# A full-height second score product and a mask on GpSimd, in the attention of a hybrid decoder layer

## The chip, the cores and the metric

The kernel runs on one core of a Trainium2 chip. The metric is the device time of one execution in microseconds (us). Its engines appear under the profile's names: PE is TensorE (matrix products; PEld is its weight load), DVE is VectorE, ACT is ScalarE, POOL is GpSimd, SP is SyncE, which issues the loads.

## What is computed

One layer of a decoder for 512 tokens of 1,024 values, all in float32: a recurrent branch, an attention branch, an MLP and a gated embedding, each with its norm. The change touches the attention alone. It has 16 heads of 64 values, is strictly causal, and weighs the keys by stick breaking:

```python
z = einsum('bhqd,bhkd->bhqk', q_blk, k) * scale          # scale = 1/8
causal = key_pos[None, :] < q_pos[:, None]
log_1m = where(causal, log_sigmoid(-z), 0.0)
suffix = cumsum(log_1m, axis=3, reverse=True) - log_1m
att = where(causal, exp(log_sigmoid(z) + suffix), 0.0)
y = einsum('bhqk,bhkd->bhqd', att, v)
```

So the weight of a key is sigmoid(z) times the product of sigmoid(-z) over all later keys that are allowed.

## The kernel before

Float32 products are made of two float32r parts per operand, a rounded high part and the exact rest (`split`, lines 53 and 54: a copy on ACT, a subtraction on DVE). A projection (`proj`) is 24 products of 128 rows by 512 columns: 8 tiles of the contraction, three products each (lines 120 to 122). The weights stream in halves of 512 KB, three buffers deep, each split one half ahead of its use.

The heads come in 8 pairs; a pair's two heads lie on partitions 0 to 63 and 64 to 127 of one projection. For each pair there is one projection of q and one of k into PSUM. All projections share three PSUM slots (pool `pp`). `qk_evac` empties them: for head j of the pair, `qs[:, j, :]` holds the high part of q on the head's own 64 partitions and the low part on the other 64 (lines 405 and 406), `kh[:, j, :]` the high part of k on both halves (lines 407 and 408), and `kl` the low part of k, both heads in one tile, each on its own partitions (line 409). These three tiles have two buffers in turn, by pair. ACT's and DVE's reads of one PSUM tile are put in the order of the code.

`scores` handles a head's queries in four blocks of 128 (`qb`), with the keys 0 to w = 128 (qb + 1). The first product (line 419) has 128 rows, (high q, low q) against (high k, high k). The second (line 420) adds high q against low k, with the head's 64 rows only. A mask tile, 0 where allowed and -1e30 elsewhere, is added to the diagonal block of z in PSUM (line 421, DVE). Then come two sigmoids, r of -z and s of z (lines 425 and 426, ACT), a scan that multiplies r up from the last key (line 427, DVE), and s times the scan (line 429, DVE). There are 16 heads of 4 blocks, so each of these lines has 64 instructions. `values` transposes the weights of the head before (line 440), splits them and multiplies them with v (lines 449 and 450). `branch_gate` adds projections for the two branch gates (`ps_gl`, `ps_ga`); those, and the q and k projections of the next pairs, are what PE issues between the small products of a head.

The order of the instructions on each engine is not written out: the framework plans it ahead of the run, by the order of the code and a model of the durations, with the dependences and the buffers that it knows.

Of the kernel before, what the change touches and what calls it, by code (L numbers as in the profile page):

```python
# [8 lines left out]
F32 = mybir.dt.float32  # L9
F32R = mybir.dt.float32r  # L10
I32 = mybir.dt.int32
AF = mybir.ActivationFunctionType
ALU = mybir.AluOpType
PSUM = bass.MemoryType.PSUM

P = 128
S = 512
D = 1024
KT = D // P
NB = S // P  # L20
FF = 4096
HEADS = 16
DH = 64
PAIRS = HEADS // 2
EPS = 1e-6
NEG = -1.0e30
GN = 4
# [5 lines left out]
def hybrid_layer(ctx, tc, xT, pT, vecs, gfin, gates, w_in, w_bl, w_ba, w_out,  # L33
                 w_up, w_dn, w_pg, w_ple, out):
    nc = tc.nc
    sc, ve, pe, gp, sy = nc.scalar, nc.vector, nc.tensor, nc.gpsimd, nc.sync
# [6 lines left out]
    def f32(ap):  # L43
        return ap.bitcast(F32)

# [1 line left out]
    def load_raw(src, name):  # L47
# [21 lines left out]

    # half chunks of weights (1024 per partition) in the order of use, each split ahead of its use  # L70
    halves = []
# [59 lines left out]

# [1 line left out]
    vt = const.tile([P, len(VECS), 8], F32, name="vt")  # L133
# [9 lines left out]
    for a, b in ((0, 1), (1, 2), (2, 4), (4, 6), (6, 8)):  # L143
# [8 lines left out]
    sc.activation(zero, onesf[:, 0:1], AF.Copy, scale=0.0)  # L152
    mask = const.tile([P, P], F32, name="mask")
    gp.memset(mask, 0.0)
    gp.affine_select(mask, mask, pattern=[[-1, P]], compare_op=ALU.is_gt, fill=NEG,
                     base=0, channel_multiplier=1)

    # keeps the tensor engine's clock up while the first loads arrive
    with tc.tile_pool(name="warm", bufs=1, space=PSUM) as pw:
# [12 lines left out]
    def row_sums(acc, pool, name):  # L172
        """sums over the partitions of acc, tokens on the partitions: [128, NB] in PSUM"""
        ps = pool.tile([P, S], F32, tag="ps", name="sum_" + name, bufs=1)
        for tb in range(NB):
            pe.matmul(ps[:, tb:tb + 1], acc[:, tb * P:(tb + 1) * P], onesf[:, 0:1],
                      start=True, stop=True)
        return ps[:, 0:NB]

    def spread(cols, pool, dpool, name):  # L180
        """a value per token, [128, NB], to every partition: [128, S] in PSUM"""
        ps = pool.tile([P, S], F32, tag="ps", name="bc_" + name, bufs=1)
        for tb in range(NB):
            dg = dpool.tile([P, P], F32, tag="dg", name=f"dg_{name}{tb}", bufs=2)
            ve.tensor_scalar(dg, ident, cols[:, tb:tb + 1], None, op0=ALU.mult)
            pe.matmul(ps[:, tb * P:(tb + 1) * P], onesf, dg, start=True, stop=True)
        return ps

    def rsqrt_cols(y, ss, pool, name, rest=None):
        """1/sqrt(ss / D + eps), a few values per partition"""  # L190
        n = y.shape[1]
        v = pool.tile([P, n], F32, tag="nv", name="v_" + name, bufs=2)
        t = pool.tile([P, n], F32, tag="nt", name="t_" + name, bufs=2)
        yi, vi = y.bitcast(I32), v.bitcast(I32)
        ve.tensor_scalar(v, ss, 1.0 / D, EPS if rest is None else rest, op0=ALU.mult, op1=ALU.add)
        ve.tensor_scalar(yi, vi, 1, None, op0=ALU.logical_shift_right)
        ve.tensor_scalar(yi, yi, -1, 0x5F1FFFF9, op0=ALU.mult, op1=ALU.add)

        def ratio():
            if n == 1:  # L200
                ve.scalar_tensor_tensor(t, y, y, v, op0=ALU.mult, op1=ALU.mult)
            else:
                ve.tensor_tensor(t, y, y, op=ALU.mult)
                ve.tensor_tensor(t, t, v, op=ALU.mult)

        ratio()
        ve.tensor_scalar(t, t, -0.703952253, 1.68191391, op0=ALU.mult, op1=ALU.add)
        ve.tensor_tensor(y, y, t, op=ALU.mult)
        ratio()
        ve.tensor_scalar(v, t, 0.375, -1.25, op0=ALU.mult, op1=ALU.add)  # L210
        ve.tensor_tensor(t, t, v, op=ALU.mult)
        return ve.scalar_tensor_tensor(y, t, 1.875, y, op0=ALU.add, op1=ALU.mult)

# [1 line left out]
    vs = big.tile([P, PAIRS, NB, 4, DH], F32R, tag="B1", name="vs")  # L215
# [58 lines left out]

# [1 line left out]
    with tc.tile_pool(name="lru", bufs=1) as lp, \  # L276
            tc.tile_pool(name="pg", bufs=3, space=PSUM) as pgp:
        # decay constants: 8 softplus(-lam)
        sp8 = const.tile([P, 8], F32, name="sp8")
# [70 lines left out]

        # u_x
        pend = None
# [13 lines left out]
        y_lru = big.tile([P, KT, S], F32, tag="F1", name="y_lru")  # L366
        # u_g
        for n in range(KT):
# [11 lines left out]

# [1 line left out]
        w = next_pair("v3")  # L382
# [4 lines left out]

# [1 line left out]
    f2 = ctx.enter_context(tc.tile_pool(name="f2", bufs=1))  # L389
    t1 = f2.tile([P, KT, S], F32, tag="F2", name="t1")  # L390
    t2 = f2.tile([P, KT, S], F32, tag="F3", name="t2")
    yas = vs.rearrange("p a t b d -> p a (t b d)").rearrange("p a (h s) -> p a h s", h=2)
    with tc.tile_pool(name="att", bufs=2) as ap, \
            tc.tile_pool(name="pz", bufs=2, space=PSUM) as pz, \
            tc.tile_pool(name="pt", bufs=2, space=PSUM) as ptp, \
            tc.tile_pool(name="py", bufs=1, space=PSUM) as pyp:

        def qk_evac(p, psq, psk):
            qs = ap.tile([P, 2, S], F32R, tag="qs", name=f"qs{p}")
            kh = ap.tile([P, 2, S], F32R, tag="kh", name=f"kh{p}")  # L400
            kl = ap.tile([P, S], F32R, tag="kl", name=f"kl{p}")
            for j in range(2):
                a = slice(j * DH, (j + 1) * DH)
                b = slice((1 - j) * DH, (2 - j) * DH)
                sc.copy(qs[a, j, :], psq[a, :])
                ve.tensor_tensor(qs[b, j, :], psq[a, :], f32(qs[a, j, :]), op=ALU.subtract)
                sc.copy(kh[a, j, :], psk[a, :])
                sc.copy(kh[b, j, :], psk[a, :])
                ve.tensor_tensor(kl[a, :], psk[a, :], f32(kh[a, j, :]), op=ALU.subtract)
            return qs, kh, kl  # L410

        turned, summed = {}, {}     # of the last head so far: last transpose and last product, by block of keys

        def scores(p, j, qb, qs, kh, kl):
            w = (qb + 1) * P
            a = slice(j * DH, (j + 1) * DH)
            q = slice(qb * P, w)
            z = pz.tile([P, S], F32, tag="z", name=f"z{p}_{j}_{qb}")
            pe.matmul(z[:, 0:w], qs[:, j, q], kh[:, j, 0:w], start=True, stop=False)
            pe.matmul(z[:, 0:w], qs[a, j, q], kl[a, 0:w], start=False, stop=True)  # L420
            ve.tensor_tensor(z[:, q], z[:, q], mask, op=ALU.add)  # L421
            r = ap.tile([P, S], F32, tag="r", name=f"r{p}_{j}_{qb}", bufs=3)
            s = ap.tile([P, S], F32, tag="s", name=f"s{p}_{j}_{qb}", bufs=6)
            pr = ap.tile([P, S], F32, tag="pr", name=f"pr{p}_{j}_{qb}", bufs=2)
            sc.activation(r[:, 0:w], z[:, 0:w], AF.Sigmoid, scale=-0.125)  # L425
            sc.activation(s[:, 0:w], z[:, 0:w], AF.Sigmoid, scale=0.125)
            ve.tensor_tensor_scan(pr[:, 0:w][:, ::-1], r[:, 0:w][:, ::-1],  # L427
                                  zero.broadcast_to([P, w]), 1.0, op0=ALU.mult, op1=ALU.add)
            ve.tensor_tensor(s[:, 0:w - 1], s[:, 0:w - 1], pr[:, 1:w], op=ALU.mult)  # L429
            return s  # L430
# [57 lines left out]

# [1 line left out]
    pools["proj"] = pq = ctx.enter_context(tc.tile_pool(name="pq", bufs=4, space=PSUM))  # L490
# [23 lines left out]

# [1 line left out]
    sumsq = big2.tile([P, S], F32, tag="S", name="sumsq2")  # L516
# [6 lines left out]

# [1 line left out]
    rs2 = sumsq  # L525
# [9 lines left out]
    for half in range(2):  # L535
# [13 lines left out]
        if half == 0:  # L549
            # p @ w_ple, token-major, between the halves  # L550
            ple = f2.tile([P, NB, D], F32, tag="F2", name="ple")
# [30 lines left out]

# [1 line left out]
    work = big2.tile([P, 8192], F32, tag="B3", name="work")  # L584
# [40 lines left out]

    # w_ple_gate, all resident: three halves in the stream's slots, five in buffers now free
    wb1 = big.tile([P, 8, 1024], F32R, tag="B1", name="wb1")
# [24 lines left out]
def _layout(a):  # L652
    """Host layout only: tiles of 128 rows, chunks that one transfer brings in whole."""
    import numpy as np
# [67 lines left out]
```

## Time and profile before

| | |
|---|---|
| median of 3 runs | 969.02 us (968.84 to 971.86) |
| span of the profiled execution | 967.4 us |
| the three runs one by one | 971.86, 969.02, 968.84 us |
| PE busy | 951.4 us (98%) |
| DVE busy | 554.4 us (57%) |
| ACT busy | 471.9 us (49%) |
| POOL busy | 5.5 us (1%) |

The span is the time from the first to the last instruction of the one execution that was profiled; a run's time is longer by what lies around it, 1.6 us from this span to the median. Times of the trace count from the span's start. A matmul's duration in the trace overlaps with the next one's, so how fast products follow each other is read from their starts. "a <-b" in a list of waits says that b released a.

### The profile page before, as it was taken

Reading aid. Unit: us, or ns where it says so; the run is one execution under the profiler, and the core shown is the slowest. Engines: PE = TensorE matmul, PEld = TensorE weight load, DVE = VectorE, ACT = ScalarE, POOL = GpSimd, SP = SyncE. Lnnn points to the kernel's source line nnn. Section 1 sums busy time; section 2 is a strip of 40 time slices with the busy share of each in tenths; the row PEclk is TensorE's granted clock in tenths of the full one; section 3 lists DMA queues with packets and bytes.
Section 4 is the critical chain, followed back from the end, with each engine's and each line's share of the span. In section 5 each row is a group of like instructions: output and inputs, shape, how many; then the busy total and the mean of one; then the engine's idle time right before and its main releaser. Section 6 shows DMA issues by size and latency. Waiting matters only on the chain.

```text
span 967.4 us, 11858 instructions
## 1 busy us (share of the span) xinstructions
PE 951.4 (98%) x4634; PEld 789.3 (82%) x4634; DVE 554.4 (57%) x882; ACT 471.9 (49%) x751; POOL 5.5 (1%) x19
## 2 busy tenths in 40 slices
PE   7999999999999999999999999999999999999996
PEld 7988888777777777788888888888888888888896
DVE  6896847688887887553555543424343333444476
ACT  6568594656565665441324355542123545333443
POOL 0000000000000000000000000000000000000000
PEclk9999999999999999999999999999999999999998
DMA  6342323212211111243223232323323232232312
GB/s 214 94 131 66 109 66 109 88 44 66 65 66 65 67 66 44 66 174 106 90 93 103 87 109 88 111 71 123 109 87 108 88 99 98 88 104 92 109 44 88
DMA packets 25400, 89.41 MB, mean 92 GB/s; under 512 B 2944, under 2 KB 3200, under 8 KB 25088
## 3 DMA queue, kind: packets, MB, share of 16 engines
q1 hardware_dynamic: 24768, 87.61, 27.3%
q10 hardware_dynamic: 576, 1.05, 0.3%
q8 instruction: 36, 0.59, 0.3%
q14 instruction: 20, 0.16, 0.1%
HBM read 86.55 MB, written 2.10 MB: 92 GB/s over the span
## 4 chain that ended last, share of the span: by engine, by line
PE 95%; ACT 2%; DVE 1%; DMA 1%; issue 1%; SPq 0%; ACTq 0%
PE ps_up L120 6%; PE dn L122 6%; PE dn L120 6%; PE ps_up L122 6%; PE ps_up L121 6%; PE dn L121 6%; PE z L420 2%; PE t L440 2%; PE ps_k L120 2%; PE ps_gl L121 2%; PE ps_q L121 2%; PE ps_k L122 2%; PE pgt L121 2%; PE pgt L122 2%; PE ps_gl L120 2%; PE pgt L120 2%
## 5 line engine op out<-in xcount | busy, mean ns | idle before, releaser
L120 PE MATMUL dn<-ah,whi_dn 128*128 128x512 f32 x256 | 100.3, 392 | 0.0
L120 PE MATMUL ps_up<-h,whi_up 128*128 128x512 f32 x256 | 100.0, 391 | 0.0
L122 PE MATMUL ps_up<-h,wlo_up 128*128 128x512 f32 x256 | 99.8, 390 | 0.0
L122 PE MATMUL dn<-ah,wlo_dn 128*128 128x512 f32 x256 | 99.8, 390 | 0.0
L121 PE MATMUL ps_up<-h,whi_up 128*128 128x512 f32 x256 | 99.7, 390 | 0.0
L121 PE MATMUL dn<-al,whi_dn 128*128 128x512 f32 x256 | 99.7, 389 | 0.0
L53 ACT CAST whi_dn<-raw_dn 128x1024 fp32r<-128x1024 f32 x32 | 33.6, 1053 | 108.4 <-PE dn L121 82.9
L54 DVE TENSOR_TENSOR wlo_up<-raw_up,whi_up 128x1024 fp32r<-128x1024 f32 x32 | 39.2, 1224 | 73.5 <-ACT whi_up L53 73.5
L53 ACT CAST whi_up<-raw_up 128x1024 fp32r<-128x1024 f32 x32 | 33.7, 1054 | 91.4 <-PE ps_up L121 63.0
L54 DVE TENSOR_TENSOR wlo_dn<-raw_dn,whi_dn 128x1024 fp32r<-128x1024 f32 x32 | 39.0, 1222 | 67.6 <-ACT whi_dn L53 67.6
L122 PEld LDWEIGHTS dn<-ah,wlo_dn 128*128 128x128 f32 x256 | 48.1, 188 | 10.1
L122 PEld LDWEIGHTS ps_up<-h,wlo_up 128*128 128x128 f32 x256 | 48.1, 188 | 10.0
L121 PEld LDWEIGHTS ps_up<-h,whi_up 128*128 128x128 f32 x256 | 48.1, 188 | 9.9
L121 PEld LDWEIGHTS dn<-al,whi_dn 128*128 128x128 f32 x256 | 48.1, 188 | 9.9
L120 PEld LDWEIGHTS ps_up<-h,whi_up 128*128 128x128 f32 x256 | 48.1, 188 | 9.8
L120 PEld LDWEIGHTS dn<-ah,whi_dn 128*128 128x128 f32 x256 | 48.1, 188 | 9.6
L427 DVE TENSOR_TENSOR_SCAN pr<-r,zero 128x128 f32<-128x128 f32 (+1 forms) x64 | 51.7, 817 | 5.1 <-ACT r L425 4.7
L425 ACT ACTIVATE r<-z 128x128 f32<-128x128 f32 (+1 forms) x64 | 28.2, 440 | 33.5 <-DVE z L421 33.3
L575 DVE TENSOR_TENSOR d<-dn,sumsq 128x512 f32<-128x512 f32 x16 | 11.1, 692 | 52.1 <-PE dn L122 52.1
L54 DVE TENSOR_TENSOR al<-rl,ah 128x512 fp32r<-128x512 f32 x32 | 22.2, 693 | 18.2 <-ACT ah L53 18.1
L421 DVE TENSOR_TENSOR z<-z,mask 128x128 f32<-128x128 f32 x64 | 18.5, 294 | 24.4 <-PE z L420 24.0
L429 DVE TENSOR_TENSOR s<-s,pr 128x127 f32<-128x127 f32 (+1 forms) x64 | 30.4, 484 | 2.6
(282 smaller groups left out, 2415.0 us busy)
## 6 DMA issues: line engine op xcount, KB each, us to landing
raw_up<-in_w_up_dram SPq DMA_DIRECT2D x32, 512.0 KB, 3.4
raw_dn<-in_w_dn_dram SPq DMA_DIRECT2D x32, 512.0 KB, 3.6
raw_u<-in_w_in_dram SPq DMA_DIRECT2D x16, 512.0 KB, 3.6
raw_qk<-in_w_in_dram SPq DMA_DIRECT2D x16, 512.0 KB, 3.4
raw_gl<-in_w_in_dram SPq DMA_DIRECT2D x8, 512.0 KB, 3.4
raw_ga<-in_w_in_dram SPq DMA_DIRECT2D x8, 512.0 KB, 3.4
raw_bl<-in_w_bl_dram SPq DMA_DIRECT2D x8, 512.0 KB, 3.6
raw_ba<-in_w_ba_dram SPq DMA_DIRECT2D x8, 512.0 KB, 3.4
```

Source lines behind the costliest of these rows:

```text
L53: sc.copy(hi, src)
L54: ve.tensor_tensor(lo, src, f32(hi), op=ALU.subtract)
L120: pe.matmul(ps, lh, rh, start=(first and i == 0), stop=False)
L121: pe.matmul(ps, lh, rl, start=False, stop=False)
L122: pe.matmul(ps, ll, rh, start=False, stop=(last and i == n - 1))
L420: pe.matmul(z[:, 0:w], qs[a, j, q], kl[a, 0:w], start=False, stop=True)
L421: ve.tensor_tensor(z[:, q], z[:, q], mask, op=ALU.add)
L425: sc.activation(r[:, 0:w], z[:, 0:w], AF.Sigmoid, scale=-0.125)
L427: ve.tensor_tensor_scan(pr[:, 0:w][:, ::-1], r[:, 0:w][:, ::-1], zero.broadcast_to([P, w]), 1.0, op0=ALU.mult, op1=ALU.add)
L429: ve.tensor_tensor(s[:, 0:w - 1], s[:, 0:w - 1], pr[:, 1:w], op=ALU.mult)
L440: turned[kbs[0]] = pe.transpose(pt[:, o:o + P], att[qb][:, kb * P:(kb + 1) * P], ident)
L575: ve.tensor_tensor(t, ps, rs2, op=ALU.mult)
```

## The change

The key's low part becomes a tile of its own shape, `kl[:, 2, S]`, one plane per head, allocated once ahead of the attention with the other head's 64 partitions set to zero. The second product takes all 128 rows. The mask tile and its addition go; in their place POOL sets the diagonal block of r to 1 and that of s to 0 where a key is not allowed, after the sigmoids. Comments and docstrings went too; those hunks are left out.

```diff
-    mask = const.tile([P, P], F32, name="mask")
-    gp.memset(mask, 0.0)
-    gp.affine_select(mask, mask, pattern=[[-1, P]], compare_op=ALU.is_gt, fill=NEG,
-                     base=0, channel_multiplier=1)
+    def strictly_before(block, fill):
+
+        gp.affine_select(block, block, pattern=[[-1, P]], compare_op=ALU.is_gt, fill=fill,
+                         base=0, channel_multiplier=1)
...
+            tc.tile_pool(name="kl", bufs=1) as kp, \
...
+        kl = kp.tile([P, 2, S], F32R, name="kl")
+        for j in range(2):
+            gp.memset(f32(kl[(1 - j) * DH:(2 - j) * DH, j, :]), 0.0)
+
         def qk_evac(p, psq, psk):
             qs = ap.tile([P, 2, S], F32R, tag="qs", name=f"qs{p}")
             kh = ap.tile([P, 2, S], F32R, tag="kh", name=f"kh{p}")
-            kl = ap.tile([P, S], F32R, tag="kl", name=f"kl{p}")
...
-                ve.tensor_tensor(kl[a, :], psk[a, :], f32(kh[a, j, :]), op=ALU.subtract)
+                ve.tensor_tensor(kl[a, j, :], psk[a, :], f32(kh[a, j, :]), op=ALU.subtract)
...
-            pe.matmul(z[:, 0:w], qs[a, j, q], kl[a, 0:w], start=False, stop=True)
-            ve.tensor_tensor(z[:, q], z[:, q], mask, op=ALU.add)
+            pe.matmul(z[:, 0:w], qs[:, j, q], kl[:, j, 0:w], start=False, stop=True)
...
             sc.activation(r[:, 0:w], z[:, 0:w], AF.Sigmoid, scale=-0.125)
+            strictly_before(r[:, q], 1.0)
             sc.activation(s[:, 0:w], z[:, 0:w], AF.Sigmoid, scale=0.125)
+            strictly_before(s[:, q], 0.0)
```

## Rows read from the trace of the kernel before

**Rows 1.** The page: the engines' busy time, and the chain that ended last.

```profile
PE 951.4 (98%) x4634; PEld 789.3 (82%) x4634; DVE 554.4 (57%) x882; ACT 471.9 (49%) x751; POOL 5.5 (1%) x19
...
PE 95%; ACT 2%; DVE 1%; DMA 1%; issue 1%; SPq 0%; ACTq 0%
```

**Rows 2.** Busy time by stretch: length, then PE, PEld, DVE, ACT, POOL, clock, DMA.

```profile
171.00:402.00 231.00, 231.00 (x1067) 177.00 (x1066) 184.11 (x317) 140.92 (x282) 0.00 (x0) 1.00 0.20 64
200.00:230.00 30.00, 30.00 (x142) 23.09 (x141) 25.98 (x45) 19.19 (x40) 0.00 (x0) 1.00 0.17 57
402.00:430.00 28.00, 27.03 (x124) 22.16 (x123) 15.25 (x21) 12.70 (x20) 0.00 (x0) 1.00 0.39 140
```

**Rows 3.** PE's timeline, 188 to 193 us: start, duration, engine, line, operation.

```profile
188.09 0.39 PE L122 MATMUL ps_gl<-hT,wlo_gl 128*128 128x512 f32 x1
...
190.81 0.39 PE L122 MATMUL ps_gl<-hT,wlo_gl 128*128 128x512 f32 x1
191.04 0.22 PE L419 MATMUL z<-kh,qs 128*128 128x128 f32 x1
191.19 0.32 PE L420 MATMUL z<-kl,qs 64*128 64x128 f32 x1
191.44 0.50 PE L120 MATMUL ps_gl<-hT,whi_gl 128*128 128x512 f32 x1
191.78 0.39 PE L121 MATMUL ps_gl<-hT,whi_gl 128*128 128x512 f32 x1
192.01 0.28 PE L419 MATMUL z<-kh,qs 128*128 128x256 f32 x1
...
192.86 0.39 PE L120 MATMUL ps_gl<-hT,whi_gl 128*128 128x512 f32 x1
```

**Rows 4.** PE's timeline, 249.8 to 250 us.

```profile
249.80 0.22 PE L449 MATMUL y<-th,vs 128*128 128x128 f32 x1
249.86 0.28 PE L450 MATMUL y<-tl,vs 128*128 128x128 f32 x1
249.97 0.39 PE L419 MATMUL z<-kh,qs 128*128 128x384 f32 x1
```

**Rows 5.** The waits, 171 to 402 us: total, times, longest.

```profile
ACT r L425 <- DVE z L421: 33.3, 22, 4.1
DVE z L421 <- PE z L420: 24.0, 25, 2.3
PEld z L420 <- issue: 13.8, 51, 0.4
...
ACT kh L407 <- DVE kl L409: 5.5, 4, 2.2
```

**Rows 6.** Line 420's instructions: durations in ns, first and last start, forms.

```profile
L420 PE MATMUL z<-kl,qs x64: 323/410/502, 176.3 to 394.0; 64*128 64x128 f32 x16, 64*128 64x256 f32 x16, 64*128 64x384 f32 x16, 64*128 64x512 f32 x16
```

**Rows 7.** The page's groups of DVE: busy us, mean ns, idle before.

```profile
L427 DVE TENSOR_TENSOR_SCAN pr<-r,zero 128x128 f32<-128x128 f32 (+1 forms) x64 | 51.7, 817 | 5.1 <-ACT r L425 4.7
...
L421 DVE TENSOR_TENSOR z<-z,mask 128x128 f32<-128x128 f32 x64 | 18.5, 294 | 24.4 <-PE z L420 24.0
L429 DVE TENSOR_TENSOR s<-s,pr 128x127 f32<-128x127 f32 (+1 forms) x64 | 30.4, 484 | 2.6
```

**Rows 8.** The groups of POOL over the whole span: busy us, mean ns.

```profile
L300 POOL MEMSET gh<- 128x2048 f32 x1 | 1.8, 1820 | 44.7 <-PE pv L122 44.7
...
L155 POOL TENSOR_SCALAR_AFFINE_SELECT mask<-mask 128x128 f32<-128x128 f32 x1 | 0.3, 292 | 0.0
```

**Rows 9.** The timelines of DVE and PE around the hand-over to pair 6.

```profile
321.21 0.69 DVE L409 TENSOR_TENSOR kl<-ps_k,kh 64x512 fp32r<-64x512 f32 x1 [0.79 <-ACT kh L408]
...
333.44 0.39 PE L120 MATMUL ps_gl<-hT,whi_gl 128*128 128x512 f32 x1
...
339.06 0.49 PE L420 MATMUL z<-kl,qs 64*128 64x512 f32 x1
...
346.51 0.69 DVE L406 TENSOR_TENSOR qs<-ps_q,qs 64x512 fp32r<-64x512 f32 x1
```

More of the change, by code (lines that the diff above doesn't have):

```diff
@@ L25 @@
 EPS = 1e-6
-NEG = -1.0e30
 GN = 4
@@ L415, in scores @@
             w = (qb + 1) * P
-            a = slice(j * DH, (j + 1) * DH)
             q = slice(qb * P, w)
```

## The prediction, made before the change was run

> **What bounds the kernel now.** I read the page's engine line first, then its chain. PE is busy for 98% of the span and holds 95% of the chain that ended last [rows 1]. So the kernel ends when PE has issued its last product, and an edit is worth what it takes out of PE's stream, or what it puts into it as idle time. The change touches only the attention stage, from 171 to 402 us. The table by stretch says what room the other engines have there [rows 2]: PE 231.0 of 231.0 us, DVE 184.1 (80%), ACT 140.9 (61%), POOL nothing; the clock is granted in full (1.00).
>
> A busy PE is not a PE at its peak, so the next view is PE's timeline, read by starts and not by durations. A run of twelve products of 512 columns, from 188.09 to 190.81, takes 2.72 us [rows 3]: 0.227 us each, 0.443 ns a column. Everything that follows is held against this cadence. The second score product (line 420, 64 rows) breaks it. At 191.04 a first product of 128 columns, a second of 128 and a projection of 512 take until 191.78, thus 0.74 us for 768 columns, which at the cadence are 0.34. At 192.01 the same three with 256, 256 and 512 columns take until 192.86, 0.85 us for what should be 0.45 [rows 3]. Both times 0.40 us are lost, whatever the width: about 0.1 ahead of the 64-row product, 0.2 behind it, 0.1 behind the next. Two 128-row products into one PSUM bank lose nothing of the kind: two value products of 128 columns and what follows them start 0.06 and 0.11 apart [rows 4]. So neither the short width, nor a new weight load, nor the shared bank is to blame; what is left is the 64 rows. The list of waits agrees: the weight load of line 420 sat idle 51 times, 13.8 us, with no engine to blame [rows 5].
>
> **The change part by part.**
>
> *128 rows in the second product.* The trace has all 64 of them, 16 of each width [rows 6]. Their columns stay as they were, and the added rows are fed zeros, so at the cadence they cost nothing new. 64 x 0.40 = 25.6 us leave PE's stream. The bounds: nothing, if the loss had another cause (a rival, below), and hardly more than 25.6, since a stage in which PE is never idle has no other PE time to give.
>
> *The mask leaves DVE.* 64 additions of 294 ns, 18.5 us [rows 7]. DVE does not bound the stage, so I count them at nothing; what they give is room. They also take one pass through DVE's queue out of the chain from scores to sigmoid: ACT had waited 33.3 us for the mask, and DVE 24.0 us for the product under it [rows 5].
>
> *128 selects come to POOL.* A select of 128x128 took 292 ns [rows 8], so 128 x 0.292 = 37.4 us on an engine that is empty in a stage of over 200. For each block the chain gains one hop, sigmoid to select to scan, in place of the mask's hop before the sigmoid. What hides it is that a head's values are formed only after the next head's scores. If that cover fails, the scan stands waiting on DVE, and behind it the splits of weights, of turned attention and of q and k, on which PE waits. The fill and the select that build the mask go, and two zero fills of 64x512 come: a fill of 2,048 columns took 1.82 us [rows 8], so about 0.46 each, on an idle engine, once.
>
> *One key tile in place of two in turn.* This is the edit with a cost that no row shows. The low parts of pair p+1 are now written into the tile that the second products of pair p read. So the subtraction of line 409 for a half must wait for the last of them, and until then the PSUM slot of the key projection stays taken. In the run of before those writes came early: for pair 6 at 321.21, while the last second product of pair 5 came at 339.06 [rows 9], 18 us later. Three such slots serve all projections, and mostly two suffice meanwhile. Where they don't is seen at that same hand-over: with the slot of key projection 6 kept, query 7 is emptied until 346.51, key 7 is projected until 333.44, and the gate projection that begins at 333.44 would want a fourth slot [rows 9]. It would come free near 340.2 (339.06 + 0.49 for the product + 0.69 for the subtraction), so 6.8 us of filler are missing. Of the seven hand-overs one more looks like it, to pair 4; I bound it by the same 6.8. Together that is 13.6 us if PE finds nothing else to issue, and 0 if the planner, which knows the slots, puts the gate projection ahead of the key. I take 4.0, nearer to nothing, because at the other one the gate projection began less than a us ahead of the last product, and because PE has scores, transposes and values to issue in those gaps. The waiting subtraction also blocks what is queued behind it on DVE, and ACT's copy of the other half, which waited for line 409 already (5.5 us in 4 waits [rows 5]).
>
> *The sum.* The profiled span is 967.4 us, 1.6 under the median of 969.0; I take that 1.6 as unchanged. 967.4 - 25.6 + 4.0 = 945.8, with the 1.6 again 947.4: I say **947.0 us**.
>
> **The rivals.**
>
> *POOL and DVE block each other (chance 0.15).* No row of before shows a select beside DVE work. The Trainium skill, on the page SBUF — State Buffer (Who interferes with whom), says that a DVE instruction with two SBUF inputs and a GpSimd instruction that reads SBUF exclude each other, the later one standing still until the first is done; by that rule the select is the wrong engine for the mask, and no run here shows it yet. In this kernel the scan (51.7 us), the product behind it (30.4 us) [rows 7] and the weight splits have both inputs in SBUF. The price, if each select holds DVE up for its whole length: DVE's 184.1 us in the stage, less 18.5 of masks, are 165.6, in a stage that 25.6 shorten to 205.4, or 81%; with 37.4 of selects they are 203.0, or 99%. In its densest stretch before, 200 to 230 us, DVE was 87% busy [rows 2]. If it can be filled to 99%, this costs nothing; if to 87% only, the stage takes 233 us and the gain is gone. Between the two, at 93%, the stage takes 218, the gain is 13, and the time 956. It decides from (0.87 x 205.4 - 165.6) / 128 = 0.10 us for each select. Against it: selects can fall beside DVE's work from PSUM, and DVE's 24.0 us of waiting for the product under the mask are gone.
>
> *The single key tile takes PE's filler away (0.12), the other side.* If at each of the 7 hand-overs one projection of 24 x 0.227 = 5.4 us can't be placed, PE loses 38 us, and the time is 969 - 25.6 + 38 = 981. It decides from 25.6 / 7 = 3.7 us a hand-over. For it: the slot would be kept longer at every one of the seven, 18 us at the one shown [rows 9]. Against it: only two of the seven had a fourth projection begun in that time.
>
> *The 128-row product loses the same 0.40 (0.07).* Then something else of line 420 breaks the cadence, the change does not do what it says, and the time stays at 969. Against it stand the value products [rows 4].
>
> **How the numbers follow.** The forecast with all its bounds has 0.66: 967.4 - 25.6 + 1.6 = 943 with no loss, 957 with 13.6 lost, and 3 us less for another order of work by the planner (PE's idle time next to the stage, from 402 to 430, is 1.0 us [rows 2]). So its own range is 940 to 957. The range of 8 in 10 takes in the blocking rival: 940 to 961; left out are the other two and the tails. A measurement of this kernel tells about 0.3%, or 2.9 us, from no change. Faster by more than that has the forecast and the blocking rival, 0.81; the same 0.07; slower 0.12.
>
> **What would show it.** In the profile after, line 420 should read 128*128, start 0.06 to 0.23 us before the next product by its width, and leave the next one on the cadence; the idle time of its weight load should be near zero. The attention stage should shrink from 231 to about 209 us, with all other stages as long as before. PE idle in the stage, released by line 405 to 409 or by a projection's slot, is the 4.0. POOL should show 128 selects near 0.29 us; if they last longer, or the scan and the product behind it go over their 817 and 484 ns [rows 7], or DVE waits for POOL by tens of us, the blocking rival holds. I am wrong if line 420 at 128 rows still costs 0.40, or if PE stands idle over 25 us in the stage.

## The result and the profile after

The changed kernel takes 946.04 us (median of 4 runs, 945.92 to 946.40); the kernel before, run beside it, 970.32. The ratio is 0.9754, with a 95% interval from 0.9738 to 0.9770: faster by 2.5%, 24.3 us. The forecast was 947.0.

The page of the kernel after, the lines that answer to [rows 1]:

```profile
PE 929.5 (98%) x4634; PEld 790.9 (84%) x4634; DVE 542.4 (57%) x818; ACT 471.3 (50%) x751; POOL 67.9 (7%) x147
...
PE 95%; ACT 2%; DVE 1%; DMA 1%; issue 1%; SPq 0%; ACTq 0%
```

PE issues the same 4,634 products in 21.9 us less busy time and is still the bound. Where the time came from shows in PE's timeline. The kernel after, from 194.31 to 195.59, answers to [rows 3]:

```profile
194.31 0.33 PE L423 MATMUL z<-kh,qs 128*128 128x384 f32 x1
194.49 0.34 PE L424 MATMUL z<-kl,qs 128*128 128x384 f32 x1
194.66 0.40 PE L120 MATMUL ps_gl<-hT,whi_gl 128*128 128x512 f32 x1
194.90 0.39 PE L423 MATMUL z<-kh,qs 128*128 128x512 f32 x1
195.12 0.40 PE L424 MATMUL z<-kl,qs 128*128 128x512 f32 x1
195.36 0.39 PE L121 MATMUL ps_gl<-hT,wlo_gl 128*128 128x512 f32 x1
195.59 0.39 PE L119 MATMUL ps_q<-hT,whi_qk 128*128 128x512 f32 x1
```

The first three products have 1,280 columns and take 0.59 us, where the cadence of 0.443 ns a column gives 0.57; the next three have 1,536 and take 0.69, where it gives 0.68. So 0.01 to 0.02 us are lost where it had been 0.40. A group whose score products have 128 columns is not so cheap:

```profile
188.83 0.22 PE L423 MATMUL z<-kh,qs 128*128 128x128 f32 x1
188.89 0.28 PE L424 MATMUL z<-kl,qs 128*128 128x128 f32 x1
189.00 0.45 PE L121 MATMUL ps_gl<-hT,wlo_gl 128*128 128x512 f32 x1
189.29 0.39 PE L119 MATMUL ps_gl<-hT,whi_gl 128*128 128x512 f32 x1
```

Its 768 columns take 0.46 us where the cadence gives 0.34: 0.12 us are still lost. The weight load of the second product (now line 424) is no longer in the list of waits, where it had stood with 13.8 us.

To see the stage by itself I read where the first query projection starts. That is at 158.23 us before and 159.48 after, in this order:

```profile
158.23 0.40 PE L120 MATMUL ps_q<-hT,whi_qk 128*128 128x512 f32 x1
```

```profile
159.48 0.40 PE L119 MATMUL ps_q<-hT,whi_qk 128*128 128x512 f32 x1
```

From there to the end of the span it is 809.2 us before and 784.5 after: 24.7 us fewer. The 1.25 us by which the projection starts later lie ahead of the attention, behind the same number of products (850), and their cause was not looked for; over the kernels below that start moves between 158.0 and 160.1 us (in one kernel, where the pool of these projections was changed, it is 166.9). So the profile is read from that start on. From 171 to 402 us TensorE's granted clock is 1.00 in the kernel before [rows 2] and in the one after.

What waits for what has turned round. The waits of the kernel after, 150 to 400 us (total, times, longest), answering to [rows 5]:

```profile
POOL r L155 <- ACT r L428: 190.2, 54, 75.2
ACT r L428 <- PE z L424: 27.0, 15, 3.4
DVE pr L432 <- POOL r L155: 10.2, 17, 2.0
DVE kl L414 <- PE z L424: 3.6, 2, 2.1
```

POOL waits for its sigmoids most of the time, DVE waits 10.2 us for the selects, and the key write (line 414) waited for the second product twice, 3.6 us. No line names PE as the one that waited in the attention stage: from the first query projection to its last product PE is never idle, where it had stood 1.0 us before.

The groups of POOL in the kernel after (busy us, mean ns) and, from its page, the scan and the product behind it, answering to [rows 7, 8]:

```profile
L155 POOL TENSOR_SCALAR_AFFINE_SELECT s<-s 128x128 f32<-128x128 f32 x64 | 33.6, 525 | 5.1 <-ACT s L430 3.3 <-PE t L445 0.4
L155 POOL TENSOR_SCALAR_AFFINE_SELECT r<-r 128x128 f32<-128x128 f32 x64 | 29.8, 466 | 192.6 <-ACT r L428 190.2 <-DVE wlo_qk L53 2.2
```

```profile
L432 DVE TENSOR_TENSOR_SCAN pr<-r,zero 128x128 f32<-128x128 f32 (+1 forms) x64 | 54.1, 845 | 10.7 <-POOL r L155 10.2
...
L434 DVE TENSOR_TENSOR s<-s,pr 128x127 f32<-128x127 f32 (+1 forms) x64 | 31.8, 498 | 3.6
```

The selects are slower than the 292 ns of the quiet start, 466 and 525 ns. DVE pays little: the scan's mean went from 817 to 845 ns, the product's from 484 to 498, in all (28 + 14) x 64 = 2.7 us.

### The profile page after: what moved, and what is told of

Same layout as the page of the kernel before. It is cut to its first block, busy times and chain, and to the rows that moved or that the text cites. A ratio compares the mean times of both kernels' runs of the same rounds, so it can differ in the third digit from the quotient of the medians.

```text
span 944.0 us, 12123 instructions
## 1 busy us (share of the span) xinstructions
PE 929.5 (98%) x4634; PEld 790.9 (84%) x4634; DVE 542.4 (57%) x818; ACT 471.3 (50%) x751; POOL 67.9 (7%) x147
## 4 chain that ended last, share of the span: by engine, by line
PE 95%; ACT 2%; DVE 1%; DMA 1%; issue 1%; SPq 0%; ACTq 0%
PE ps_up L119 6%; PE dn L121 6%; PE ps_up L121 6%; PE dn L119 6%; PE dn L120 6%; PE ps_up L120 6%; PE t L445 2%; PE pgt L120 2%; PE pgt L121 2%; PE pgt L119 2%; PE ps_gl L121 2%; PE ps_k L121 2%; PE ps_q L119 2%; PE ps_ga L121 2%; PE ps_q L120 2%; PE ps_k L119 2%
## 5 line engine op out<-in xcount | busy, mean ns | idle before, releaser
L432 DVE TENSOR_TENSOR_SCAN pr<-r,zero 128x128 f32<-128x128 f32 (+1 forms) x64 | 54.1, 845 | 10.7 <-POOL r L155 10.2
L155 POOL TENSOR_SCALAR_AFFINE_SELECT r<-r 128x128 f32<-128x128 f32 x64 | 29.8, 466 | 192.6 <-ACT r L428 190.2
L155 POOL TENSOR_SCALAR_AFFINE_SELECT s<-s 128x128 f32<-128x128 f32 x64 | 33.6, 525 | 5.1 <-ACT s L430 3.3
```

Source lines behind the costliest of these rows:

```text
L155: gp.affine_select(block, block, pattern=[[-1, P]], compare_op=ALU.is_gt, fill=fill, base=0, channel_multiplier=1)
```

## The experiments

All nine kernels in one table. The second column is the ratio to the kernel before with its interval. The next four are of each one's profiled execution: the start of the first query projection, the span, the time from that start to the end, and PE's idle time between that start and its last product (1.0 us before). The last is the difference of the time from that start, taken before rounding, from the 809.2 of before.

| kernel | ratio to before | first q, us | span, us | from there | PE idle | difference |
|---|---|---|---|---|---|---|
| the change | 0.9754 (0.9738 to 0.9770) | 159.48 | 944.0 | 784.5 | 0.0 | -24.7 |
| rows128_mask_dve | 0.9774 (0.9753 to 0.9796) | 158.03 | 945.2 | 787.2 | 1.9 | -22.0 |
| rows64_mask_pool | 0.9982 (0.9971 to 0.9993) | 158.27 | 965.2 | 806.9 | 0.0 | -2.2 |
| three_key_planes | 0.9741 (0.9724 to 0.9758) | 160.14 | 944.6 | 784.5 | 0.0 | -24.7 |
| selects_twice | 0.9744 (0.9727 to 0.9761) | 159.59 | 944.3 | 784.7 | 0.0 | -24.5 |
| rows64_cut_in_two | 1.0078 (1.0063 to 1.0093) | 158.77 | 975.4 | 816.6 | 2.1 | +7.5 |
| two_slots | 0.9854 (0.9838 to 0.9871) | 166.87 | 954.8 | 787.9 | 2.2 | -21.2 |
| fill_beside_select | 0.9736 (0.9716 to 0.9755) | 158.07 | 942.6 | 784.5 | 0.0 | -24.6 |
| dve_load_back | 0.9757 (0.9742 to 0.9771) | 159.03 | 945.9 | 786.9 | 0.8 | -22.3 |

**rows128_mask_dve: the rows alone.** Against the changed kernel:

```diff
+    mask = const.tile([P, P], F32, name="mask")
...
+            ve.tensor_tensor(z[:, q], z[:, q], mask, op=ALU.add)
...
-            strictly_before(r[:, q], 1.0)
...
-            strictly_before(s[:, q], 0.0)
```

> The 128-row product with its padded key tile alone; the mask stays an addition on DVE ahead of the sigmoids. My theory, that the 64-row products cost PE 0.40 us each and that the place of the mask is worth nothing: 946 us, within 3 (ratio 0.973 to 0.979), and line 420's successor starting on the cadence. The rival, that the gain came from the mask leaving DVE's queue (18.5 us of additions, 33.3 us of ACT's waits): 965 to 970.

Measured: 949.06 us. The rows give 22.0 us of the 24.7, so the rival that the mask made the gain falls. But the time is at the upper end of what I expected, and 2.7 us of the gain are missing. Its PE timeline, and the DVE work that PE waited for:

```profile
318.12 0.40 PE L423 MATMUL z<-kl,qs 128*128 128x512 f32 x1
318.33 0.27 DVE L424 TENSOR_TENSOR z<-z,mask 128x128 f32<-128x128 f32 x1
318.63 0.69 DVE L461 TENSOR_TENSOR yf<-y,yf 64x512 f32<-64x512 f32 x1
...
319.48 0.47 PE L452 MATMUL y<-th,vs 128*128 128x512 f32 x1 [0.96 <-DVE yf L461]
...
320.15 0.69 DVE L413 TENSOR_TENSOR kl<-ps_k,kh 64x512 fp32r<-64x512 f32 x1
...
320.89 0.50 PE L120 MATMUL ps_gl<-hT,whi_gl 128*128 128x512 f32 x1 [0.95 <-DVE kl L413]
```

With PE's stream shortened and the masks still on DVE, PE stands twice, 1.9 us in all: once for the emptying of y, queued behind a mask, and once for the PSUM slot that a key write frees. The second, 0.95 us, looks like the wait that the prediction feared of the single key tile, but it is only in part that: the last second product that this key write had to wait for was done at 318.52 (318.12 + 0.40), 1.6 us ahead of the write. The copy of the high part that it subtracts came from ACT at 319.41, and a product and a mask stood ahead of it in DVE's queue.

**rows64_mask_pool: the mask alone.** Against the changed kernel:

```diff
-            pe.matmul(z[:, 0:w], qs[:, j, q], kl[:, j, 0:w], start=False, stop=True)
+            a = slice(j * DH, (j + 1) * DH)
+            pe.matmul(z[:, 0:w], qs[a, j, q], kl[a, j, 0:w], start=False, stop=True)
```

> The changed kernel with one edit undone: the second product takes 64 rows again, out of the same padded key tile; selects stay on POOL. My theory: the 25.6 us come back, 970 to 974 us, with about 0.1, 0.2 and 0.1 us lost around each product. The rival, that the mask's move made the gain: 946 to 950.

Measured: 968.36 us, just under the range that I gave: from the first query projection on, the mask's move alone is worth 2.2 us. The loss around the product is back (its PE timeline):

```profile
194.93 0.33 PE L423 MATMUL z<-kh,qs 128*128 128x384 f32 x1
195.19 0.44 PE L425 MATMUL z<-kl,qs 64*128 64x384 f32 x1
195.56 0.50 PE L120 MATMUL ps_gl<-hT,whi_gl 128*128 128x512 f32 x1
195.90 0.40 PE L423 MATMUL z<-kh,qs 128*128 128x512 f32 x1
```

1,280 columns take 0.97 us from 194.93 to 195.90, where the changed kernel took 0.59 for the same ones. The two parts add up: 22.0 + 2.2 = 24.2 of the 24.7. With the selects in place, the rows are worth 806.9 - 784.5 = 22.4 us, or 0.35 a product.

**rows64_cut_in_two: what the 64 rows cost.** Against the kernel before:

```diff
-            pe.matmul(z[:, 0:w], qs[a, j, q], kl[a, 0:w], start=False, stop=True)
+            pe.matmul(z[:, 0:w // 2], qs[a, j, q], kl[a, 0:w // 2], start=False, stop=False)
+            pe.matmul(z[:, w // 2:w], qs[a, j, q], kl[a, w // 2:w], start=False, stop=True)
```

> The kernel before with each second product cut into two 64-row products of half the columns, one behind the other; columns and result stay the same. If the loss sits at the change between 128 and 64 rows, the added product pays only what a 64-row product right behind a 64-row one pays; at the one place of the trace of before where two of them follow each other (176.27 to 176.69, two of 128 columns) that is 0.11 us more than for a single one, so 64 x 0.11 = 7 us at most: 970 to 977 us. If each 64-row product pays its own 0.3 to 0.4 us, whatever stands ahead of it: 64 x 0.3 to 0.4 = 19 to 26 us, 989 to 996 us.

Measured: 978.33 us, 7.7 over the kernel before it was compared with (970.64): 1.3 above the first range that I gave, and far below the second. From the first query projection on it is 7.5 us. Its PE timeline, two groups:

```profile
191.71 0.22 PE L419 MATMUL z<-kh,qs 128*128 128x128 f32 x1
191.86 0.29 PE L420 MATMUL z<-kl,qs 64*128 64x64 f32 x1
191.99 0.27 PE L421 MATMUL z<-kl,qs 64*128 64x64 f32 x1
192.19 0.50 PE L120 MATMUL ps_gl<-hT,whi_gl 128*128 128x512 f32 x1
192.53 0.28 PE L419 MATMUL z<-kh,qs 128*128 128x256 f32 x1
...
213.17 0.39 PE L419 MATMUL z<-kh,qs 128*128 128x512 f32 x1
213.49 0.38 PE L420 MATMUL z<-kl,qs 64*128 64x256 f32 x1
213.72 0.28 PE L421 MATMUL z<-kl,qs 64*128 64x256 f32 x1
213.92 0.50 PE L122 MATMUL ps_k<-hT,wlo_qk 128*128 128x512 f32 x1
214.26 0.40 PE L120 MATMUL ps_q<-hT,whi_qk 128*128 128x512 f32 x1
```

In the first group the same 768 columns as in [rows 3], with one product more, take 0.82 us in place of 0.74. In the second, 1,536 columns take 1.09 us where the cadence gives 0.68: 0.41 are lost, no more than with a single 64-row product. So the loss is paid at the change from 128 rows to 64 and back, once per group. A 64-row product right behind another adds 0.08 us where the two have 64 columns each, and nothing where they have 256.

The 7.5 us are therefore not 64 equal shares. 1.1 of them are idle time of PE (2.1 us against 1.0). And in 9 of the 64 blocks the planner put another product between the two halves, so that the change is paid twice: in the group from 205.64 to 206.67 us, 768 columns take 1.03 us, and 0.69 are lost.

The Trainium skill says on its page TensorEngine Tiling (Array Packing), Key Properties, that a change of tiling mode drains TensorE. That agrees with the 0.40 us of a group and with the second group above, which loses no more for two 64-row products than others for one.

**three_key_planes: the single key tile.** Against the changed kernel:

```diff
-        kl = kp.tile([P, 2, S], F32R, name="kl")
+        kl = kp.tile([P, 3, S], F32R, name="kl")
...
-                ve.tensor_tensor(kl[a, j, :], psk[a, :], f32(kh[a, j, :]), op=ALU.subtract)
+                ve.tensor_tensor(kl[a, j * (1 + p % 2), :], psk[a, :], f32(kh[a, j, :]), op=ALU.subtract)
...
-            pe.matmul(z[:, 0:w], qs[:, j, q], kl[:, j, 0:w], start=False, stop=True)
+            pe.matmul(z[:, 0:w], qs[:, j, q], kl[:, j * (1 + p % 2), 0:w], start=False, stop=True)
```

> The changed kernel with a third plane in the key tile: the second head of a pair has two planes in turn by pair, so its key write waits no longer for the pair before. The first head keeps one plane. If the single tile costs what I put down for it (4.0 us), the time falls to 942 or 943. If it costs 1 us or less, which the stage of the changed kernel suggests (it shrank by 24.6 us of the 25.6), 945 to 946, ratio to the changed kernel 0.999 to 1.000. DVE's wait in the key write for the second product (3.6 us, twice) should go.

Measured: 945.85 us, 784.5 from the first query projection on, the same as the change. DVE's wait in the key write for the second product is gone from the list, and it bought nothing. The first head of a pair still has one plane; but PE is never idle in the changed kernel, so there is no wait left that a plane for it could take away. With the selects on POOL the single tile costs nothing that can be measured.

**two_slots: why not.** Against the changed kernel:

```diff
-    pp = ctx.enter_context(tc.tile_pool(name="pp", bufs=3, space=PSUM))
+    pp = ctx.enter_context(tc.tile_pool(name="pp", bufs=2, space=PSUM))
```

> The changed kernel with two PSUM slots for projections in place of three. My theory of why the single key tile cost next to nothing is that with three slots two are left while the key's is kept. Then with two, one is left, a projection can't start while the one before is emptied, and the attention stage (233.6 us from the first query projection to the first branch projection) grows by 10 to 40 us. If slots never mattered here, the stage stays within 2 us. Other stages use the same pool and may grow too, so the stage is read by itself.

Measured: 956.42 us, but most of that lies ahead of the stage: the first query projection starts at 166.87, 7.4 us later than in the changed kernel. From there on it is 787.9 - 784.5 = 3.4 us more. (The first branch projection, by which the expectation measured the stage, is no mark here: the planner put one gate projection behind it.) So neither expectation holds: a slot less costs the stage something, but a third of the least that I gave. The waits of PE in this kernel behind the start of the first query projection:

```profile
PE ps_gl L119 <- ACT t L470: 0.7, 1, 0.7
PE y L454 <- DVE yf L463: 0.7, 1, 0.7
PE y L455 <- DVE tl L53: 0.6, 1, 0.6
```

One wait of 0.7 us for a slot, even with two of them; PE's idle time as a whole makes 2.2 of the 3.4 us. My picture, that PE's filler stands or falls with the free slots, is too strong: the planner, which knows them, orders the work so that it fits.

**selects_twice: the cover on POOL.** Against the changed kernel:

```diff
-        gp.affine_select(block, block, pattern=[[-1, P]], compare_op=ALU.is_gt, fill=fill,
-                         base=0, channel_multiplier=1)
+        for _ in range(2):
+            gp.affine_select(block, block, pattern=[[-1, P]], compare_op=ALU.is_gt, fill=fill,
+                             base=0, channel_multiplier=1)
```

> The changed kernel with each select done twice (256 in place of 128; the second changes nothing). POOL's selects go from 63 us to about 126 in a stage of some 205 us. If the cover holds, as I think: 946 to 949. If selects hold DVE up for their length, each of the 128 added ones costs DVE 0.3 to 0.5 us, 38 to 64 us in all, and with some 30 us of room left in the stage the time is 956 to 980.

Measured: 946.31 us, no difference from the change. Its groups of POOL:

```profile
L156 POOL TENSOR_SCALAR_AFFINE_SELECT s<-s 128x128 f32<-128x128 f32 x128 | 66.2, 518 | 5.4 <-ACT s L431 2.9
L156 POOL TENSOR_SCALAR_AFFINE_SELECT r<-r 128x128 f32<-128x128 f32 x128 | 54.9, 429 | 135.8 <-ACT r L429 131.0 <-DVE s L435 1.9
```

121 us of selects, 58 more than in the change, cost nothing: the cover holds with much to spare, and the blocking rival falls.

**fill_beside_select: who is held up.** Against the changed kernel:

```diff
             strictly_before(r[:, q], 1.0)
+            gp.memset(pr[:, q], 0.0)
```

> The changed kernel with one more POOL instruction for each block: a fill of the scan's own 128x128 output block, which the scan then overwrites. A fill writes and reads nothing. In the changed kernel selects beside a DVE instruction with two SBUF inputs took 0.60 us on the mean, the others 0.33. If it is their reading that is held up, the fills keep the 0.204 us that a 128x128 fill took at the quiet start of the run, while the selects stay near 0.5. If POOL is slow beside DVE whatever it does, fills take 0.35 to 0.45. Time: 946 to 949.

Measured: 945.05 us (2 runs), just under the range. Its groups of POOL:

```profile
L155 POOL TENSOR_SCALAR_AFFINE_SELECT r<-r 128x128 f32<-128x128 f32 x64 | 32.5, 508 | 55.2 <-ACT r L428 54.9
L155 POOL TENSOR_SCALAR_AFFINE_SELECT s<-s 128x128 f32<-128x128 f32 x64 | 32.4, 506 | 2.8 <-ACT s L431 1.8
L430 POOL MEMSET pr<- 128x128 f32 x64 | 13.1, 206 | 126.7 <-DVE s L435 71.4 <-DVE y_lru L379 55.2
```

The fills, which only write, kept their quiet length (206 ns); the selects, which read too, took 507. Half of the fills, 32, did run beside a DVE instruction with two SBUF inputs, and they took 205 ns on the mean. So it is the reading of the selects that is held up.

**dve_load_back: where the mask's 2 us come from.** Against the changed kernel, behind the scan:

```diff
+            ve.tensor_scalar(r[:, 0:w], r[:, 0:w], 1.0, None, op0=ALU.mult)
             ve.tensor_tensor(s[:, 0:w - 1], s[:, 0:w - 1], pr[:, 1:w], op=ALU.mult)
```

> The changed kernel with DVE given 64 instructions back, behind the scan: r multiplied by 1 in place, nobody waits for it. The mask's move alone was worth about 2 us of the attention stage. If that was DVE's load (PE held up by DVE's late work on y and k), the load brings 1 to 3 us back: 947 to 949. If it was the mask's place ahead of the sigmoids, nothing comes back: 946, within 0.5.

Measured: 947.04 us; from the first query projection on 786.9, 2.4 more than the change. The 64 instructions added 21.3 us of DVE work, about the 18.5 of the masks. Of the 2.4 us, 0.5 lie behind PE's last product (9.1 us from its end to the end of the span, against 8.6); about 1.8 remain for the stage, near the 2.2 that the mask's move alone gave. The interval of the whole time (0.9742 to 0.9771) holds the change's 0.9754, so only the profile tells the two apart. The waits of PE in the stage, which the changed kernel does not have:

```profile
PE t L446 <- DVE s L435: 0.7, 1, 0.7
PE z L423 <- ACT s L430: 0.2, 1, 0.2
```

So work on DVE does cost PE time here, though DVE does not bound the stage. It is not shown that the masks cost it in the same way: the added instruction stands in DVE's queue just ahead of the product that makes s (line 435), and PE waited for that product, whereas a mask stood ahead of the sigmoids.

## Why the prediction was right

*The main step held.* The 64-row product was the cause, and its price was read from the starts of PE's products in the trace of before. The term was 25.6 us; measured it is 22.4 (22.0 without the selects), 0.35 a product in place of 0.40. The term was too large because it let the new product follow on the cadence at every width. At 256, 384 and 512 columns it nearly does (0.01 to 0.02 us lost), but a group with 128 columns still loses 0.12, and there are 16 of them: 16 x 0.12 = 1.9 us of the missing 3.2. [rows 4] had a hint of it: two value products of 128 columns, read there as losing nothing of the kind, started 0.06 and 0.11 apart, where the cadence gives 0.06 both times. For the other 1.3 us, 0.03 for each of the 48 wider blocks, I have no single line.

*The key tile was mis-sized.* I put down 4.0 us, and the third plane shows that it costs nothing measurable. The step that failed is that the gate projection "would want a fourth slot": it took the times of the kernel before as fixed. There that projection began at 333.44, 5.6 us ahead of the last second product of pair 5 [rows 9]. In the changed kernel the planner has the scores earlier among the projections, and the same gate projection begins 6.6 us behind that product:

```profile
313.91 0.39 PE L424 MATMUL z<-kl,qs 128*128 128x512 f32 x1
...
320.55 0.40 PE L119 MATMUL ps_gl<-hT,whi_gl 128*128 128x512 f32 x1
```

Two slots in all cost the stage 3.4 us. With the masks still on DVE, PE did wait once for a slot that a key write frees, 0.95 us; that write came 1.6 us behind the second product that it had to wait for.

*The mask was counted at nothing and gave 2.2 us.* The step was "DVE does not bound the stage, so I count them at nothing". On average it does not; but PE had stood 0.9 us for DVE's y just behind the stage, inside the 1.0 us of idle time in [rows 2]:

```profile
PE y L449 <- DVE yf L458: 0.9, 1, 0.9
```

It stands 1.9 us when the rows are widened and the masks stay, and not at all when the masks are gone. So idle time of PE is 1.0 of the 2.2 us; the rest is the same products issued in another order, without idle time. That the masks caused that wait through DVE's load is argued and not shown: the last of them ended at 396.24, 6 us ahead of it, and y was emptied behind a weight split. What is shown is the sum: moving 18.5 us of work off an engine that is 80% busy moved the end by about a tenth of their length.

The wrong terms partly cancel: 25.6 - 4.0 = 21.6 was the forecast from the stage, 22.4 + 2.2 = 24.6 the sum of the parts, 24.7 the measured one. That the whole time came out 1 us from the forecast is partly luck. Of the 3.1 us by which the stage gained more, 1.25 went to the later start of the changed kernel, 0.5 to what lies around its span (2.1 us in place of 1.6), and 0.4 had been rounded off the forecast's sum of 947.4.

*The rivals.* The single key tile as a loss of 38 us: nothing of it is seen. The 128-row product with the same loss: refuted by the timeline of the kernel after, and by rows64_mask_pool, where the loss comes back with the 64 rows. The blocking rival: its mechanism is there, its price is not. The Trainium skill's rule (SBUF — State Buffer, Who interferes with whom) agrees with the trace in which instructions disturb each other: of the changed kernel's 128 selects, 91 ran beside a DVE instruction with two SBUF inputs and took 0.58 us on the mean, the 37 others 0.30, and fills were not held up. Which side stands still was the open point, and here it is mostly POOL. 58 selects that began while such an instruction ran took 0.69 us; 47 such DVE instructions that began while a select ran took only 0.06 us longer than the same ones before, though the select had 0.26 us left on the mean. An extreme case from the changed kernel:

```profile
206.17 0.68 DVE L463 TENSOR_TENSOR yf<-y,yf 64x512 f32<-64x512 f32 x1
206.22 1.59 POOL L155 TENSOR_SCALAR_AFFINE_SELECT s<-s 128x128 f32<-128x128 f32 x1
206.78 0.94 DVE L432 TENSOR_TENSOR_SCAN pr<-r,zero 128x384 f32<-128x384 f32 x1
```

A select takes 0.29 us in a quiet stretch; this one takes 1.59 and ends at 207.81, shortly after the scan (207.72), while the scan of 384 columns keeps its length (0.94, against a mean of 0.95 for that width before). Why it was not done by 206.51, ahead of the scan and beside an instruction with one input in PSUM, stays open. I had priced the side that doesn't pay: POOL had the time, since it is idle for over two thirds of the stage.

## What to carry to other kernels

Where PE is the bound, read its timeline by starts and hold every product against the cadence of its columns: a loss that no duration and no busy share shows was worth 2.3% here, and rows padded with zeros cost less than the change between 64 and 128 rows, the least with products of 256 columns and more. Several 64-row products in a row share that price, so grouping them is the second choice where padding has no room. Before pricing a shared resource, ask which side of it has slack; and don't read the price of a lost buffer from the old times where a planner makes a new order.

## What the runs showed that was not expected

A select on POOL beside DVE work took 0.58 us in place of 0.29, and DVE's own instructions hardly changed (scan 817 to 845 ns); doubling the selects to 121 us of POOL time left the kernel at 946.31 us. Cutting the 64-row product in two added nothing to the 0.41 us that a group of 512 columns loses; a narrow 128-row product, of 128 columns, is what still leaves the cadence after the change.
